# Accumulators in turn, earlier loads and pinned weight sums in the up projection of a decoder layer

## The chip, the core and the metric

The kernel runs on one core of a Trainium2 chip. The core has a matmul engine (PE, with its weight loads shown apart as PEld), a vector engine (DVE), an activation engine (ACT), a general engine (POOL, also called GpSimd) and a queue engine (SP) that issues transfers from device memory. Matmul results go to PSUM, here used as eight tiles of 128 x 512 float32 values (eight banks); PE writes them, and DVE and ACT read them. POOL reads and writes only the on-chip memory SBUF in this kernel. The metric is the device time of one execution in microseconds; lower is better. A comparison is by the median of several executions.

## What is computed

One decoder layer on 512 tokens of 1024 values: an RMS norm, two parallel token mixers (RWKV-7 and a sparse attention) with gates and an output projection, and then a gated MLP. The change lies in the first half of the MLP alone:

```python
h = rms_norm(x, norm_ffn_pre[l])
u = causal_dwconv(h @ ffn_up[l], ffn_conv_w[l], ffn_conv_b[l])
u_gate, u_val = jnp.split(u, 2, axis=-1)
x = x + rms_norm((jax.nn.silu(u_gate) * u_val) @ ffn_down[l], norm_ffn_post[l])
```

`ffn_up` is 1024 x 5632, which is 44 blocks of 128 output channels; the convolution is causal, three tokens wide, and runs on each channel by itself.

## The kernel before

**Precision.** A float32 product is made of three products in PE's faster format: each operand is split into a high part and the residue that the high part leaves, and high x high, high x low and low x high are added up in one accumulator. A split costs one copy on ACT (the high part) and one subtraction on POOL or DVE (the residue). `split_to` (L157) and `split_w` (L165) load a weight block from device memory in two halves through SP's queue and split them: copy on ACT (listed under L125), residue on POOL (L163). The raw halves, the high parts and the residues each have three buffers (WB = 3), so that about one and a half blocks of weights are held.

**The up stage.** The loop over `j` (L1592) takes 22 pairs of blocks; blocks 2j and 2j+1 are the gate and the value channels of one slice. For an ordinary block, `mm3` (L220 to L224) runs 24 matmuls of 512 columns into one accumulator `pu`, taken by `pj` from a ring of two. Blocks 0 to 2 are begun before the loop (`half_up`), in other accumulators. After each block come its convolution steps: an ACT pass with scale and bias (L1619) and two DVE passes that add the shifted tokens (L1620, L1621). All three read the accumulator, and the ring gives it to the next block but one only when they are done. After a pair come SiLU on ACT (L1625), the gated product on POOL (L1626), and the split of the product for the down projection on ACT and DVE (L1627, L1628).

**Half products.** For the pairs j = 7, 9, ..., 19 (`SEVEN`) the two blocks are not multiplied directly. `seven` (L1548) cuts the product of two weight blocks and the tokens into quarters and forms it with seven quarter-size products instead of eight (Winograd's scheme): 84 matmuls of 256 columns, into three accumulators named sg, sv and st from `px`, `py` and `pz`, rings of two each. Each of the seven products is a call of `prod` (L1559 to L1564). Three take plain weight quarters, split by `plain` (L1549 to L1554, into the buffers that ordinary blocks use); four take sums and differences of weight quarters, made by `seven_prep` (L1519 to L1546): four transfers of raw quarters `q` through SP's queue, four DVE passes (L1534, L1537, L1541, L1544), each followed by an ACT copy (L1530) and a DVE residue (L1531). Between products, DVE adds partial results (L1567); the add into `u2` reads the left half of st, whose right half is the target of the fourth product, and an accumulator is tracked as a whole. The token operands of the sums are the token forms (`token_forms`, L1483 to L1517), made once on DVE and ACT during blocks 4 to 11.

`seven_prep` is a generator that the loop advances: its loads and first sum are traced at the start of pair j - 1, the others after blocks of that pair.

**What sets the order.** The code is traced in program order, and a planner then writes a fixed order for each engine: going through time by its own cost estimates, an engine takes the ready instruction that was traced first. So an instruction whose inputs the planner believes to be there early is placed ahead of earlier traced ones that still wait. On the chip each engine runs its own list strictly in that order and waits where an input is late. `tc.keep_in_program_order(i)` binds instruction i to stand behind the one traced before it on its engine; instructions traced later may still be placed ahead of it. SBUF and PSUM buffers are given out in turn by tag, and the first write waits for the last reader of the buffer's previous content.

Of the kernel before, what the change touches and what calls it, by code (L numbers as in the profile page):

```python
# [10 lines left out]
F32 = mybir.dt.float32  # L11
F32R = mybir.dt.float32r
AF = mybir.ActivationFunctionType
OP = mybir.AluOpType
# [13 lines left out]
SEVEN = tuple(range(7, 20, 2))  # L28
# [15 lines left out]
def hybrid_layer(ctx: ExitStack, tc: tile.TileContext, a, out, dbg=None, stop=None):  # L44
    nc = tc.nc
    te, ve, sc, po, sy = nc.tensor, nc.vector, nc.scalar, nc.gpsimd, nc.sync

    def pool(name, side="left", c=None):
        p = tc.tile_pool(name=name, bufs=1, side=side, reuse_waits="tile")
        if c is None:  # L50
            return p
        return c.enter_context(p)
# [6 lines left out]
    def pj(name):  # L59
        return ps.tile([128, 512], F32, tag="pj", name=name, bufs=2)  # L60

    def px(name):
        return ps.tile([128, 512], F32, tag="px", name=name, bufs=2)

    def py(name):
        return ps.tile([128, 512], F32, tag="py", name=name, bufs=2)
# [11 lines left out]
    def pz(name):  # L78
        return pzs[-1][1].tile([128, 512], F32, tag="pz", name=name, bufs=2)
# [85 lines left out]
    def split_w(src, name, late=False):  # L165
        hs, ls = [], []
        for i in range(2):
            hi = wp.tile([128, 512], F32R, tag="whi", name=f"{name}h{i}", bufs=WB)
            lw = wp.tile([128, 512], F32R, tag="wlo", name=f"{name}l{i}", bufs=WB)
            split_to(src[:, i * 512:i * 512 + 512], hi, lw, f"{name}{i}", 512, late=late)  # L170
            hs.append(hi)
            ls.append(lw)
        return hs, ls
# [46 lines left out]
    def mm3(p, wh, wl, mh, ml, n=KT, first=True, last=True):  # L220
        for k in range(n):
            te.matmul(p, wh(k), mh(k), start=first and k == 0, stop=False)  # L222
            te.matmul(p, wh(k), ml(k), start=False, stop=False)  # L223
            te.matmul(p, wl(k), mh(k), start=False, stop=last and k == n - 1)  # L224
# [703 lines left out]
    for g in range(2):  # L928
        group_tiles(g)
        for i in range(GP):  # L930
            p = GP * g + i
# [326 lines left out]
    for p8 in range(8):  # L1258
        v = values(p8, os_[p8])
        s = score(p8 + 1, os_[p8 + 1]) if p8 < 7 else iter(())  # L1260
# [142 lines left out]
    op = pool("op", "left", octx)  # L1403
# [40 lines left out]
    def half_up(b, half):  # L1444
        wh, wl = (wslice(w) for w in up4[b])
        ts = slice(half * 256, half * 256 + 256)
        p = pu4[b][:, ts]
        for k in range(KT):
            te.matmul(p, wh(k), h2h[:, k, ts], start=k == 0, stop=False)
            te.matmul(p, wh(k), h2l[:, k, ts], start=False, stop=False)  # L1450
            te.matmul(p, wl(k), h2h[:, k, ts], start=False, stop=k == KT - 1)  # L1451
# [20 lines left out]
    with pool("ff") as ff:  # L1472
# [7 lines left out]
        def quarter(t, r, c):  # L1480
            return t[:, r * hf:(r + 1) * hf, (lft, rgt)[c]]
# [34 lines left out]
                    low(3, (1, 0))  # L1516
                    yield  # L1517

        def seven_prep(j, sw):  # L1519
            o = P()  # L1520
            o.raw = {}
            for r, c in ((1, 0), (1, 1), (0, 0), (0, 1)):
                q = o.raw[r, c] = sw.tile([128, 512], F32, tag=f"q{r}{c}", name=f"q{j}{r}{c}", bufs=1)
                sy.dma_start(q, a["up"][2 * j + r][:, c * 512:c * 512 + 512])
            s = sw.tile([128, 512], F32, tag="qs", name=f"qs{j}", bufs=1)
            o.w = {}

            def put(i, q):
                hi, lo = (sw.tile([128, 512], F32R, tag=f"s{i}{x}", name=f"s{j}{i}{x}", bufs=1) for x in "hl")
                sc.activation(hi, q, AF.Copy)  # L1530
                ve.tensor_tensor(lo, q, hi.bitcast(F32), op=OP.subtract)  # L1531
                o.w[i] = hi, lo

            ve.tensor_tensor(s, o.raw[1, 0], o.raw[1, 1], op=OP.add)  # L1534
            put(1, s)
            yield o
            ve.tensor_tensor(s, s, o.raw[0, 0], op=OP.subtract)  # L1537
            put(2, s)
            yield o
            q = o.raw[1, 0]  # L1540
            ve.tensor_tensor(q, o.raw[0, 0], q, op=OP.subtract)  # L1541
            put(3, q)
            yield o
            ve.tensor_tensor(s, o.raw[0, 1], s, op=OP.subtract)  # L1544
            put(4, s)
            yield o  # L1546

        def seven(j, o):  # L1548
            def plain(r, c, eng):  # L1549
                hi = wp.tile([128, 512], F32R, tag="whi", name=f"ph{j}{r}{c}", bufs=WB)  # L1550
                lo = wp.tile([128, 512], F32R, tag="wlo", name=f"pl{j}{r}{c}", bufs=WB)
                sc.activation(hi, o.raw[r, c], AF.Copy)  # L1552
                eng.tensor_tensor(lo, o.raw[r, c], hi.bitcast(F32), op=OP.subtract)  # L1553
                return hi, lo  # L1554

            def tok(r, c):
                return quarter(h2h, r, c), quarter(h2l, r, c)

            def prod(p, w, x, first=True, last=True):  # L1559
                for k in range(hf):  # L1560
                    ks = slice(k * 128, k * 128 + 128)
                    for n, (y, z) in enumerate(((0, 0), (0, 1), (1, 0))):
                        te.matmul(p, w[y][:, ks], x[z][:, k, :], start=first and k + n == 0,  # L1563
                                  stop=last and k == hf - 1 and n == 2, skip_group_check=True)  # L1564

            def add(o_, x, y):
                ve.tensor_tensor(o_, x, y, op=OP.add)  # L1567

            g, v, t = px(f"sg{j}"), py(f"sv{j}"), pz(f"st{j}")
            w11 = plain(0, 0, po)  # L1570
            prod(g[:, lft], w11, tok(0, 0))
            prod(t[:, lft], o.w[2], forms[1])
            u2, u4 = (sw.tile([128, 256], F32, tag=f"u{i}", name=f"su{i}{j}", bufs=1) for i in (2, 4))
            sc.activation(u2, g[:, lft], AF.Copy)
            add(u2, t[:, lft], u2)
            prod(v[:, rgt], o.w[1], forms[0])
            add(u4, v[:, rgt], u2)
            w12 = plain(0, 1, po)
            prod(t[:, rgt], o.w[3], forms[2])
            prod(g[:, lft], w12, tok(1, 0), first=False)  # L1580
            add(v[:, rgt], t[:, rgt], u4)
            prod(g[:, rgt], o.w[4], tok(1, 1))
            add(g[:, rgt], g[:, rgt], u4)
            w22 = plain(1, 1, ve)
            prod(t[:, rgt], w22, forms[3], first=False)
            add(v[:, lft], t[:, rgt], u2)
            return g, v

        side = tf = token_forms()
        sctx2 = ExitStack()  # L1590
        nxt = None
        for j in range(22):  # L1592
            us = []
            sv_ = None
            if j in SEVEN:
                for _ in side:
                    pass
                sv_ = seven(j, nxt)
            elif j + 1 in SEVEN:
                if j + 1 == SEVEN[0]:  # L1600
                    for _ in side:
                        pass
                    sw = pool("sw", "right", sctx2)
                side = seven_prep(j + 1, sw)
                nxt = next(side)
            for x in range(2):
                blk = 2 * j + x
                if blk < NU:
                    p = pu4[blk]
                    half_up(blk, 1)  # L1610
                elif sv_ is not None:
                    p = sv_[x]
                else:
                    wh, wl = after.get(blk) or split_w(a["up"][blk], f"up{blk}")
                    p = pj(f"pu{blk}")
                    mm3(p, wslice(wh), wslice(wl), lambda k: h2h[:, k, :], lambda k: h2l[:, k, :])
                cv = blk * 4
                u = ff.tile([128, S], F32, tag=f"u{x}", name=f"u{blk}", bufs=2)
                sc.activation(u, p, AF.Identity, scale=cvec[:, cv + 2:cv + 3], bias=cvec[:, cv + 3:cv + 4])  # L1619
                ve.scalar_tensor_tensor(u[:, 1:], p[:, :S - 1], cvec[:, cv + 1:cv + 2], u[:, 1:], op0=OP.mult, op1=OP.add)  # L1620
                ve.scalar_tensor_tensor(u[:, 2:], p[:, :S - 2], cvec[:, cv:cv + 1], u[:, 2:], op0=OP.mult, op1=OP.add)  # L1621
                us.append(u)
                if j > 1:
                    next(side, None)
            sc.activation(us[0], us[0], AF.Silu)  # L1625
            po.tensor_tensor(us[1], us[0], us[1], op=OP.mult)  # L1626
            sc.activation(ah[:, j, :], us[1], AF.Copy)  # L1627
            ve.tensor_tensor(al[:, j, :], us[1], ah[:, j, :].bitcast(F32), op=OP.subtract)  # L1628
            if j == 1:
                f4ctx.close()  # L1630
# [120 lines left out]
```

## Time and profile before

Three executions gave 1166.04, 1166.78 and 1168.3 us; the median is 1166.78.

| what | value |
|---|---|
| profiled execution, its own time | 1167.55 us |
| its span, first to last instruction | 1165.7 us |
| mean granted matmul clock over the span | 0.994 |
| PE busy | 1138.4 us |
| DVE busy | 657.4 us |
| ACT busy | 604.5 us |
| POOL busy | 539.6 us |

How to read the rows that follow in the prediction. A timeline row has the start, the duration, engine, line, operation, output <- input, shape and count; brackets give the engine's idle time just before and the event that ended it, as far as the profile can tell. A row of waits has who waited for whom: total, number of times, longest. A windows row has the stretch, its length, the busy time of PE, PEld, DVE, ACT and POOL, each with its number of instructions, the granted clock, the share of the transfer engines and GB/s. A group row has line, engine, operation, names, shapes and count, then the busy total in us, the mean of one in ns, and the idle time before them. Durations of matmuls overlap, so their pace is read from their starts. Releasers are inferred; where the engine named had long been done, it was another.

### The profile page before, as it was taken

The numbers are of one execution on the slowest core, as the hardware profiler recorded it, in microseconds if no ns is written. First come the engines' busy times: TensorE is split into PE (matmuls) and PEld (weight loads), VectorE is DVE, ScalarE is ACT, GpSimd is POOL, SyncE is SP. The second block draws the span as 40 slices with busy tenths as digits, with TensorE's granted clock in tenths as the row PEclk, the third lists the DMA queues.
The fourth block names the chain that finished last, engine by engine and source line by source line (L and its number), as shares of the span: only waits on it lengthen the run. The fifth ranks groups of instructions, "written<-read, shape, count | busy, mean of one in ns | idle before, by whom it ended". The sixth has DMA issues, their size and how long they took to land. (4 is left out here: it accounts for less than half of the span.)

```text
span 1165.7 us, 20396 instructions
## 1 busy us (share of the span) xinstructions
PE 1138.4 (98%) x7590; PEld 922.1 (79%) x7590; DVE 657.4 (56%) x1316; ACT 604.5 (52%) x1194; POOL 539.6 (46%) x516
## 2 busy tenths in 40 slices
PE   9999999999999999999999999999899999999997
PEld 7888887777888777667777778889678888888886
DVE  4246656735664833787887646556856766631103
ACT  6447664545665442676766644435444555543311
POOL 4346655335754533475454334302564345454430
PEclk9999999999999999899999999999999999999999
DMA  7422345322434752244622146611333233134421
GB/s 261 109 74 80 104 112 167 94 79 85 136 105 121 199 155 88 69 116 139 198 83 73 46 154 208 229 37 37 117 95 100 82 105 100 56 112 140 128 64 73
DMA packets 95509, 131.98 MB, mean 113 GB/s; under 512 B 34033, under 2 KB 36913, under 8 KB 95154
## 3 DMA queue, kind: packets, MB, share of 16 engines
q1 hardware_dynamic: 79554, 116.26, 33.0%
q10 hardware_dynamic: 15856, 14.42, 3.9%
q8 instruction: 60, 0.98, 0.4%
q14 instruction: 39, 0.32, 0.1%
HBM read 108.30 MB, written 19.14 MB: 109 GB/s over the span
## 5 line engine op out<-in xcount | busy, mean ns | idle before, releaser
L1121 ACT ACTIVATE p<-p,stt 128x384 f32<-128x384 f32 (+3 forms) x128 | 70.7, 554 | 35.4 <-DVE stt L1119 35.1
L1119 DVE CUSTOM_DVE_ANT_0 p<-s,rh 128x384 f32<-128x384 f32 (+3 forms) x128 | 59.2, 484 | 22.7 <-PE s L1105 18.9
L1093 POOL TENSOR_SCALAR p<-p,stt 128x512 f32<-128x512 f32 (+1 forms) x64 | 39.4, 627 | 40.5 <-DVE stt L1086 24.8
L141 PE MATMUL pt<-ident,p 128*128 128x128 f32 x320 | 44.7, 275 | 1.2 <-DVE p L1095 1.2
L141 PEld LDWEIGHTS pt<-ident,p 128*128 128x128 f32 x320 | 38.0, 141 | 6.8 <-DVE p L1095 1.6
L1112 PE MATMUL s<-kst,qs 128*128 128x512 f32 (+1 forms) x128 | 39.1, 397 | 2.4 <-DVE stt L1119 2.1
L1173 PE MATMUL o<-PT,vt 128*64 128x384 f32 (+3 forms) x256 | 41.0, 443 | 0.0
L1627 ACT ACTIVATE ah<-u 128x512 fp32r<-128x512 f32 x22 | 13.9, 632 | 46.5 <-POOL u L1626 46.5
L1620 DVE SCALAR_TENSOR_TENSOR u<-pu,cvec,u 128x511 f32<-128x511 f32 x30 | 22.4, 747 | 24.5 <-ACT u L1619 24.4
L1628 DVE TENSOR_TENSOR al<-u,ah 128x512 fp32r<-128x512 f32 x22 | 16.8, 765 | 33.4 <-ACT ah L1627 32.9
L1626 POOL TENSOR_TENSOR u<-u,u 128x512 f32<-128x512 f32 x22 | 29.8, 1353 | 10.6 <-DVE u L1621 9.6
L1095 DVE TENSOR_SCALAR p<-p,stt 128x512 f32<-128x512 f32 (+1 forms) x64 | 32.7, 537 | 0.7
L1164 ACT ACTIVATE PT<-pt 128x512 f32<-128x512 f32 x48 | 27.4, 587 | 10.4 <-PE pt L141 10.2
L1173 PEld LDWEIGHTS o<-PT,vt 128*64 128x64 f32 x256 | 16.3, 136 | 18.4 <-issue 16.1
L1112 PEld LDWEIGHTS s<-kst,qs 128*128 128x128 f32 x128 | 21.5, 191 | 11.1 <-DVE stt L1119 7.7
L1395 DVE TENSOR_TENSOR p2ss<-p2ss 128x1 f32<-128x1 f32 x4 | 0.6, 160 | 52.1 <-ACT p2jl L1393 52.1
L1166 DVE COPY PT<-pt 128x512 f32<-128x512 f32 x32 | 21.8, 681 | 8.6 <-PE pt L141 8.6
L1619 ACT ACTIVATE u<-pu,cvec 128x512 f32<-128x512 f32 x30 | 22.9, 763 | 3.0 <-PE pu L1451 3.0
L1121 ACT ACTIVATION_READ_ACCUMULATOR p<-p,stt 128x1 f32 x128 | 24.3, 190 | 0.0
L824 ACT ACTIVATE UV<-xs 64x256 f32<-64x256 f32 x16 | 6.0, 378 | 35.0 <-PE xs L819 34.6
L1621 DVE SCALAR_TENSOR_TENSOR u<-pu,cvec,u 128x510 f32<-128x510 f32 x30 | 22.4, 746 | 0.8
L1625 ACT ACTIVATE u<-u 128x512 f32<-128x512 f32 x22 | 13.9, 630 | 17.1 <-DVE u L1621 17.1
(1884 smaller groups left out, 4157.7 us busy)
## 6 DMA issues: line engine op xcount, KB each, us to landing
q<-in_up_dram SPq DMA_DIRECT2D x28, 256.0 KB, 2.9
gtd<-gt ACTq DMA_DIRECT2D x16, 256.0 KB, 2.2
qs<-qd SPq DMA_DIRECT2D x32, 128.0 KB, 3.4
g<-gtd SPq DMA_DIRECT2D x16, 256.0 KB, 3.0
xt<-in_x_dram SPq DMA_DIRECT2D x4, 512.0 KB, 5.8
bvd<-bv SPq DMA_DIRECT2D x8, 256.0 KB, 2.3
t<-oad SPq DMA_DIRECT2D x8, 256.0 KB, 2.9
x<-in_x_dram SPq DMA_DIRECT2D x4, 512.0 KB, 6.8
```

The source lines that it names most:

```text
L141: return te.transpose(o, i, ident)
L1093: po.tensor_scalar(o.pe[e, b, k], o.pe[e, b, k], w, 1.0, op0=OP.mult, op1=OP.mult)
L1095: ve.tensor_scalar(o.pe[e, b, k], o.pe[e, b, k], w, None, op0=OP.mult)
L1112: m = te.matmul(s_[:, :n], qt, kt[:, x, b, :n], start=x == 0, stop=x == 1)
L1119: ve.tensor_tensor_reduce(sb, parts[b], rh[e][:, (3 - qb) * 128:], -1.0, BIG, OP.add, OP.min, st[e][:, 0, i:i + 1])
L1121: sc.activation(sb, sb, AF.Exp, scale=-1.0, bias=st[e][:, 0, i:i + 1], accum_out=st[e][:, 1, i:i + 1])
L1164: sc.activation(m[e][:, :c], pt[:, :c], AF.Copy)
L1173: te.matmul(acc[e * 64:e * 64 + 64, j * 128:], vt[:, j, b * 256 + g * 64:b * 256 + g * 64 + 64], m[e][:, c:c + n], start=False, stop=k == ...
L1619: sc.activation(u, p, AF.Identity, scale=cvec[:, cv + 2:cv + 3], bias=cvec[:, cv + 3:cv + 4])
L1620: ve.scalar_tensor_tensor(u[:, 1:], p[:, :S - 1], cvec[:, cv + 1:cv + 2], u[:, 1:], op0=OP.mult, op1=OP.add)
L1621: ve.scalar_tensor_tensor(u[:, 2:], p[:, :S - 2], cvec[:, cv:cv + 1], u[:, 2:], op0=OP.mult, op1=OP.add)
L1626: po.tensor_tensor(us[1], us[0], us[1], op=OP.mult)
```

## The change

Four things are edited, in two functions and the loop.

- Ordinary up blocks with j < 7, that is blocks 3 to 13, take their accumulators from `pj`, `px`, `py` and `pz` in turn (two buffers each) and no longer from `pj` alone. From pair 7 on, ordinary blocks use `pj` as before.
- The loads of the raw quarters are a function of their own, `seven_load`. For the first group they are traced at the start of pair 6, as before; for a later group inside the group before it, behind the plain splits, not at the start of the pair between.
- The plain splits of a group are all traced at its start, and the third residue runs on POOL, not on DVE.
- The four sums are pinned with `keep_in_program_order`, and traced in two pairs. For the first group: sums 1 and 2 after block 12's convolution steps, sums 3 and 4 after block 13's. For later groups: sums 1 and 2 after the convolution steps of the group before, sums 3 and 4 after those of the block that follows it.

```diff
-        def seven_prep(j, sw):
+        def seven_load(j, sw):
             o = P()
-            o.raw = {}
-            for r, c in ((1, 0), (1, 1), (0, 0), (0, 1)):
+            o.raw, o.w = {}, {}
+            for r, c in ((1, 0), (0, 0), (0, 1), (1, 1)):
                 q = o.raw[r, c] = sw.tile([128, 512], F32, tag=f"q{r}{c}", name=f"q{j}{r}{c}", bufs=1)
                 sy.dma_start(q, a["up"][2 * j + r][:, c * 512:c * 512 + 512])
+            return o
+
+        def seven_prep(j, o, sw):
             s = sw.tile([128, 512], F32, tag="qs", name=f"qs{j}", bufs=1)
-            o.w = {}
-            def put(i, q):
+            def put(i, q, x, y, op):
+                tc.keep_in_program_order(ve.tensor_tensor(q, x, y, op=op))
                 hi, lo = (sw.tile([128, 512], F32R, tag=f"s{i}{x}", name=f"s{j}{i}{x}", bufs=1) for x in "hl")
                 sc.activation(hi, q, AF.Copy)
-                ve.tensor_tensor(lo, q, hi.bitcast(F32), op=OP.subtract)
                 o.w[i] = hi, lo
-            ve.tensor_tensor(s, o.raw[1, 0], o.raw[1, 1], op=OP.add)
-            put(1, s)
-            yield o
-            ve.tensor_tensor(s, s, o.raw[0, 0], op=OP.subtract)
-            put(2, s)
-            yield o
+                return ve.tensor_tensor(lo, q, hi.bitcast(F32), op=OP.subtract)
+            put(1, s, o.raw[1, 0], o.raw[1, 1], OP.add)
+            put(2, s, s, o.raw[0, 0], OP.subtract)
+            yield
             q = o.raw[1, 0]
-            ve.tensor_tensor(q, o.raw[0, 0], q, op=OP.subtract)
-            put(3, q)
-            yield o
-            ve.tensor_tensor(s, o.raw[0, 1], s, op=OP.subtract)
-            put(4, s)
-            yield o
+            put(3, q, o.raw[0, 0], q, OP.subtract)
+            put(4, s, o.raw[0, 1], s, OP.subtract)
+            yield
...
             g, v, t = px(f"sg{j}"), py(f"sv{j}"), pz(f"st{j}")
-            w11 = plain(0, 0, po)
+            w11, w12, w22 = (plain(r, c, po) for r, c in ((0, 0), (0, 1), (1, 1)))
+            nxt = seven_load(j + 2, sw) if j + 2 in SEVEN else None
             prod(g[:, lft], w11, tok(0, 0))
...
-            w12 = plain(0, 1, po)
...
-            w22 = plain(1, 1, ve)
...
-                sv_ = seven(j, nxt)
+                *sv_, nxt = seven(j, cur)
             elif j + 1 in SEVEN:
                 if j + 1 == SEVEN[0]:
                     for _ in side:
                         pass
                     sw = pool("sw", "right", sctx2)
-                side = seven_prep(j + 1, sw)
-                nxt = next(side)
+                    nxt = seven_load(j + 1, sw)
+                    cur, side = nxt, seven_prep(j + 1, nxt, sw)
...
-                    p = pj(f"pu{blk}")
+                    p = ((pj, px, py, pz)[blk % 4] if j < SEVEN[0] else pj)(f"pu{blk}")
...
+            if j in SEVEN and nxt:
+                cur, side = nxt, seven_prep(j + 2, nxt, sw)
+                next(side)
```

More of the change, by code (lines that the diff above doesn't have):

```diff
@@ L1583, in seven @@
             add(g[:, rgt], g[:, rgt], u4)
-            w22 = plain(1, 1, ve)
             prod(t[:, rgt], w22, forms[3], first=False)
             add(v[:, lft], t[:, rgt], u2)
-            return g, v
+            return g, v, nxt
         side = tf = token_forms()
```

## The prediction

> **What bounds the kernel now.** I read the page first, then the waits of the matmul engine in the up stage, then that engine's timeline row by row, and last the other engines' rows around each stall.
>
> ```profile
> PE 1138.4 (98%) x7590; PEld 922.1 (79%) x7590; DVE 657.4 (56%) x1316; ACT 604.5 (52%) x1194; POOL 539.6 (46%) x516
> ```
>
> PE is busy for 98% of the span, so only its stalls can be won, unless work leaves it; the change adds and removes no matmul. The edited code runs from about 796 to 1040 us. PE's waits there:
>
> ```profile
> PE pu L222 <- DVE u L1621: 5.6, 4, 2.9
> PE st L1563 <- DVE su L1567: 2.7, 6, 0.5
> PE sg L1563 <- POOL pl L1553: 2.1, 5, 0.4
> PE pu L222 <- ACT tf1h L1497: 1.7, 2, 1.0
> ```
>
> The first and fourth rows are up blocks ahead of the half products, the others lie inside the half products. Idle time understates a stall, because each matmul is drawn with its overlapping tail, so I measure stalls by starts. **Stage A**, blocks 5 to 13:
>
> ```profile
> 817.55 0.47 PE L222 MATMUL pu<-hh,up5h 128*128 128x512 f32 x1 [0.72 <-ACT tf1h L1497]
> 824.97 0.47 PE L222 MATMUL pu<-hh,up6h 128*128 128x512 f32 x1 [1.71 <-DVE u L1621]
> 831.68 0.47 PE L222 MATMUL pu<-hh,up7h 128*128 128x512 f32 x1 [0.98 <-ACT tf1h L1497]
> 837.82 0.47 PE L222 MATMUL pu<-hh,up8h 128*128 128x512 f32 x1 [0.46 <-DVE u L1621]
> 846.45 0.47 PE L222 MATMUL pu<-hh,up9h 128*128 128x512 f32 x1 [2.94 <-DVE u L1621]
> 850.39 0.63 PE L224 MATMUL pu<-hh,up9l 128*128 128x512 f32 x1
> 854.26 0.47 PE L222 MATMUL pu<-hh,up10h 128*128 128x512 f32 x1 [0.49 <-DVE u L1621]
> 870.66 0.39 PE L222 MATMUL pu<-hh,up13h 128*128 128x512 f32 x1
> 876.10 0.28 PE L1563 MATMUL sg<-hh,ph 128*128 128x256 f32 x1
> ...
> 816.68:876.10 59.42, 52.12 (x217) 41.40 (x217) 40.14 (x49) 28.31 (x47) 33.46 (x24) 0.97 0.33 105
> 876.10:885.85 9.75, 9.75 (x85) 9.75 (x84) 8.06 (x13) 5.09 (x9) 2.90 (x3) 1.00 0.27 82
> ```
>
> Block 13 takes 876.10 - 870.66 = 5.44 us, undisturbed. Nine such blocks are 48.96 us; the first windows row shows 59.42 from the end of block 4 to the first half product. Stage A loses 10.46 us. Its costliest stall is the 2.94 before block 9; after it the matmuls run slow for a while (0.63 instead of 0.39 each, up to the row at 850.39), and the window's granted clock is 0.97. The second windows row is the first group of half products, 84 matmuls in 9.75 us without a stall: 1.39 us for each of the seven products.
>
> **Stage B**, the other six groups of half products, one example (seven 11 and the blocks ahead of it):
>
> ```profile
> 907.60 0.40 PE L222 MATMUL pu<-hh,up20h 128*128 128x512 f32 x1
> 918.51 0.28 PE L1563 MATMUL sg<-hh,ph 128*128 128x256 f32 x1
> 919.33 0.38 PE L1563 MATMUL sg<-hh,pl 128*128 128x256 f32 x1 [0.43 <-POOL pl L1553]
> 923.96 0.39 PE L1563 MATMUL st<-tf2h,s113h 128*128 128x256 f32 x1 [0.45 <-DVE su L1567]
> 929.72 0.40 PE L222 MATMUL pu<-hh,up24h 128*128 128x512 f32 x1
> ```
>
> From 918.51 to 929.72 are 11.21 us against 9.75: 1.46 lost, about 0.72 at each bracket. The PE waits count five of the first kind and six of the second. So the first kind is worth 5 x 0.72 = 3.6 us and the second 6 x 0.73 = 4.4. All stalls that the change can reach: 10.46 + 8.0 = 18.5 us.
>
> **Accumulators in turn (blocks 3 to 13).** No instruction is added. Now block n waits until the convolution steps (L1620, L1621) have read block n-2; afterwards block n-8, so the six stalls lose their cause. What is late next are the weights, which pass through ACT (high part) and POOL (residue), in queues that also hold the gated product (L1626) and its copy (L1627), which wait for DVE's convolutions:
>
> ```profile
> 822.32 1.29 POOL L163 TENSOR_TENSOR up6l<-up60r,up6h 128x512 fp32r<-128x512 f32 x1 [2.54 <-issue]
> 829.03 1.30 POOL L163 TENSOR_TENSOR up7l<-up70r,up7h 128x512 fp32r<-128x512 f32 x1 [3.74 <-issue]
> 835.57 1.64 POOL L163 TENSOR_TENSOR up8l<-up80r,up8h 128x512 fp32r<-128x512 f32 x1 [1.87 <-PE pu L224]
> ...
> 842.95 0.69 DVE L1534 TENSOR_TENSOR qs<-q,q 128x512 f32<-128x512 f32 x1 [5.28 <-DMA q<-in_up_dram]
> ```
>
> The first residue of block 6 is ready at 823.61, of block 7 at 830.33, of block 8 at 837.21. With these kept, block 8 starts at 837.21 instead of 837.82: the early stalls give almost nothing, since DVE's backlog of token forms reaches PE through the weights. The row at 842.95 shows what made the largest stall: DVE stood 5.28 us at the first sum of weight quarters, waiting for a transfer, with block 7's convolution behind it. That sum moves behind block 12 (below) and the accumulators are there, so from block 8 on nothing holds PE: 837.21 + 6 x 5.44 = 869.85 for the first half product, against 876.10. Gain 6.2. Lower bound 3, if the weights after block 8 wait once more for about that long; upper bound 10.46, if the planner, which sees PE run earlier, also puts the weights earlier. I take 6.2, the value the rows give with the order kept.
>
> **Sums pinned.** The four sums of a group and their splits are the same eight DVE and four ACT instructions as before; only their place moves. A DVE pass costs 0.68, an ACT copy 0.62:
>
> ```profile
> L1537 DVE TENSOR_TENSOR qs<-qs,q 128x512 f32<-128x512 f32 x5 | 3.4, 680 | 0.0
> L1552 ACT ACTIVATE ph<-q 128x512 fp32r<-128x512 f32 x18 | 11.1, 617 | 0.0
> ...
> 872.03 0.75 DVE L1620 SCALAR_TENSOR_TENSOR u<-pu,cvec,u 128x511 f32<-128x511 f32 x1 [0.68 <-ACT u L1619]
> 877.47 0.75 DVE L1620 SCALAR_TENSOR_TENSOR u<-pu,cvec,u 128x511 f32<-128x511 f32 x1
> ```
>
> For group 7 they come late. The last row is block 13's convolution, 1.37 us after the first half product starts; in the new kernel sums 3 and 4 follow it. It ends about 2.9 after the start; sum 3, its copy and its residue take 0.68 + 0.62 + 0.68, so the residue is there at 4.9. The fourth product is due at 3 x 1.39 = 4.17 and wants the residue 0.25 later: 0.5 us of new wait, 1.0 with one of these passes held up by POOL. I take 1.0 (bounds 0 and 3, the latter if sum 2's residue, wanted at 1.6 and behind block 12's convolution at 872.03, is late too).
>
> From group 9 on, sums 1 and 2 follow the previous group's own convolutions, sums 3 and 4 the next block's. Now they stand ahead of those convolutions:
>
> ```profile
> L1619 ACT ACTIVATE u<-pu,cvec 128x512 f32<-128x512 f32 x30 | 22.9, 763 | 3.0 <-PE pu L1451 3.0
> ...
> 913.45 0.75 DVE L1621 SCALAR_TENSOR_TENSOR u<-sv,cvec,u 128x510 f32<-128x510 f32 x1
> 915.38 1.29 POOL L1626 TENSOR_TENSOR u<-u,u 128x512 f32<-128x512 f32 x1
> 916.71 0.63 ACT L1627 ACTIVATE ah<-u 128x512 fp32r<-128x512 f32 x1 [2.70 <-POOL u L1626]
> 917.99 2.54 POOL L1553 TENSOR_TENSOR pl<-q,ph 128x512 fp32r<-128x512 f32 x2 [1.32 <-issue]
> ...
> 923.50 0.41 DVE L1567 TENSOR_TENSOR su<-st,su 128x256 f32<-128x256 f32 x1
> ```
>
> The group ended on PE at 907.60, its last convolution on DVE at 914.20. POOL's product, ACT's copy and the first plain weight's residue follow, at 919.28, where PE waits. With the sums behind, the convolution is done about 3.1 us after PE (an add 0.41, ACT 0.76, two passes of 0.75, and 0.4 between, an estimate from the gaps of these rows), so this whole chain comes 3.5 us earlier and the first kind of wait goes: 3.6 us gained. Lower bound 0, if the planner keeps the plain copy behind the same work.
>
> The second kind: the add of 923.50 must release the bank before the fourth product. Count from 907.60: convolutions to 3.1, sums 1 and 2 with copies 3.96 to 7.1, block 20's convolution to 8.6, sums 3 and 4 to 12.6, block 21's to 14.1, the add to 14.5. Due at 10.88 + 4.17 = 15.05. Slack half a microsecond, less than one held-up pass. I take half of the present wait: 2.2 us gained, bounds +4.4 and a loss (the slower rival).
>
> **Third plain residue on POOL, loads mid-group.** Seven residues move from DVE (0.69) to POOL (1.29):
>
> ```profile
> L1553 POOL TENSOR_TENSOR pl<-q,ph 128x512 fp32r<-128x512 f32 x12 | 15.2, 1291 | 7.9 <-issue 7.9
> L1553 DVE TENSOR_TENSOR pl<-q,ph 128x512 fp32r<-128x512 f32 x6 | 4.2, 692 | 7.7 <-ACT ph L1552 7.7
> 907.95:930.07 22.12, 21.24 (x134) 18.95 (x133) 15.62 (x25) 11.67 (x21) 10.21 (x9) 1.00 0.32 96
> ```
>
> POOL goes from 10.2 to 11.5 of 22 us, and that weight serves the last product only, so it costs nothing by itself; with no cover it would be 7 x 1.29 = 9. The four loads of a group pass SP's queue during the previous group, where the fourth can stand until the third residue is done; up weights are issued behind it. I price that at nothing, bounds 0 and one 1.29 per group. The gain is the transfer that DVE no longer waits for, already counted.
>
> Against this move speaks a pair of rows:
>
> ```profile
> 929.72 1.29 POOL L163 TENSOR_TENSOR up24l<-up241r,up24h 128x512 fp32r<-128x512 f32 x1 [4.58 <-ACT up24h L125]
> 929.82 1.73 DVE L1544 TENSOR_TENSOR qs<-q,qs 128x512 f32<-128x512 f32 x1
> ```
>
> A DVE pass of 0.68 that starts while POOL works ends only after it: 1.05 more. [...]
>
> **Sum.** 6.2 - 1.0 + 3.6 + 2.2 = 11.0 us. The profiled execution took 1167.55 (span 1165.7 and 1.85 around it), giving 1156.55; it lay 0.77 above the median of the runs, 1166.78, from which the sum gives 1155.8. I say **1156.0**.
>
> **Rivals.** (1) Everything goes: 18.5 less 1.0 is 17.5, so 1149. For it: PE's work is untouched; against: the weight rows above. (2) The wait only changes its name: weights in stage A leave 3 of the gain, the second wait of stage B stays whole, group 7 loses 1.0: 3 - 1.0 + 3.6 = 5.6, less a further 1.5 if the second wait grows by a quarter microsecond a group: 1162.7. For it: the DVE backlog in the weight rows. (3) Slower: sums 3 and 4 delay the bank's release. Place: DVE between the convolution of the block after a group and the add at L1567. If all four passes there are held up by POOL (4 x 1.05 = 4.2 against a slack of 0.5), PE waits 3.7 instead of 0.73 in each of six groups: 17.8 lost, against 6.2 + 3.6 - 1.0 = 8.8 kept, so 9.0 slower: 1175.8. With n held-up passes a group waits 1.05 n - 0.5; at two that is 1.6, worse than now, and it eats all gains from 2.2 us a group, between two and three passes. For it: the half microsecond; against: DVE is busy 15.62 us in 22.12, and a pass can be fitted in while ACT copies. (4) It does not do what it says: the planner hoists other work before the pins and the stalls return elsewhere: 1166.8.
>
> **How the numbers follow.** The forecast 0.48, rival 1 0.17, rival 2 0.20, rival 3 0.08, rival 4 0.07. About 0.2%, 2.3 us, is what a measurement of this kernel tells from no change. So faster 0.85, same 0.07, slower 0.08. The range from 1148.5 to 1163 leaves out rivals 3 and 4 and the tails.
>
> **What would show it.** Right: no wait of PE for L1621 in up5 to up10, only waits for residues (L163) up to block 8; the first half product near 870; its group longer than 9.75 by about 1; later groups without the wait for L1553 and with a smaller one for L1567. Wrong: stalls of 2 us or more left before block 9, later groups longer than 11.2, or a wait for the quarters' sums (s3) in every group.

## The result and the profile after

The changed kernel takes **1178.37 us** (median of five executions, 1174.61 to 1181.03); the kernel before took 1167.13 beside it (1166.04 to 1168.3). The ratio is 1.0095, with a 95% interval from 1.0069 to 1.0121: about 11 us slower, where 11 us faster was forecast. The profiled execution took 1178.37 (span 1176.6), against 1167.55 (span 1165.7).

Lines of the edited part have shifted: in the changed kernel the products are L1560 (L1563 before), the adds L1564 (L1567), the convolution steps L1615 to L1617 (L1619 to L1621), the gated product and its split L1625 to L1627, the sums L1531, their copies L1533 and residues L1535, the plain copies and residues L1549 and L1550.

The page's line of busy time, and the three longest of PE's waits from 796 to 1050 us, of the changed kernel:

```profile
PE 1141.1 (97%) x7590; PEld 923.6 (78%) x7590; DVE 656.8 (56%) x1309; ACT 606.4 (52%) x1194; POOL 560.3 (48%) x523
```

```profile
PE st L1560 <- DVE su L1564: 16.4, 6, 3.0
PE pu L224 <- POOL up8l L163: 1.0, 1, 1.0
PE st L1560 <- ACT s73h L1533: 1.0, 1, 1.0
```

All four waits that the prediction started from have changed. The two ahead of the half products and the one for `pl` are gone. The one for the add into `su` has grown from 2.7 to 16.4, as often as before.

Where the time lies is read from the first matmul of block 3 (ahead of it, executions differ by up to 4 us in a stretch that the edits do not touch). PE's timeline, chosen rows of the kernel before and then of the changed one; `dn` is the first matmul of the down projection:

```profile
805.78 0.40 PE L222 MATMUL pu<-hh,up3h 128*128 128x512 f32 x1
...
1039.89 0.39 PE L1347 MATMUL dn<-dnw00h,ah 128*128 128x512 f32 x1
```

```profile
806.46 0.40 PE L222 MATMUL pu<-hh,up3h 128*128 128x512 f32 x1
870.27 0.28 PE L1560 MATMUL sg<-hh,ph 128*128 128x256 f32 x1
909.16 0.40 PE L222 MATMUL pu<-hh,up20h 128*128 128x512 f32 x1
920.07 0.28 PE L1560 MATMUL sg<-hh,ph 128*128 128x256 f32 x1
924.11 0.28 PE L1560 MATMUL sv<-tf0h,s111l 128*128 128x256 f32 x1
927.05 0.39 PE L1560 MATMUL st<-tf2h,s113h 128*128 128x256 f32 x1 [2.67 <-DVE su L1564]
932.80 0.40 PE L222 MATMUL pu<-hh,up24h 128*128 128x512 f32 x1
1050.45 0.39 PE L1347 MATMUL dn<-dnw00h,ah 128*128 128x512 f32 x1
```

Stage A, from block 3 to the first half product, takes 870.27 - 806.46 = 63.8 us, where the kernel before took 876.10 - 805.78 = 70.3: **6.5 gained**. From there to the down projection are 180.2 us, against 163.8: **16.4 lost**. The stall before the fourth product of group 11 is the row at 927.05. Stretches of the changed kernel (group 7 with block 16, and the groups 9, 11 and 19):

```profile
870.27:888.68 18.41, 16.28 (x110) 14.56 (x108) 13.30 (x19) 8.30 (x14) 8.50 (x7) 1.00 0.33 101
894.12:909.16 15.04, 11.67 (x86) 11.27 (x84) 9.44 (x14) 6.84 (x12) 7.19 (x5) 0.89 0.28 88
920.07:932.80 12.73, 10.06 (x86) 9.87 (x84) 7.38 (x12) 5.91 (x10) 6.54 (x5) 1.00 0.34 104
1014.63:1028.66 14.03, 11.36 (x86) 11.16 (x84) 7.47 (x12) 5.91 (x10) 6.53 (x5) 0.88 0.07 20
```

Group 7 and block 16 took 9.75 + 5.44 = 15.2 before, so 3.2 are lost there. Groups 11 to 17 take 12.73 each instead of 11.21. Group 19 takes 1.3 more again, at a granted clock of 0.88; group 9 takes 2.3 more, at 0.89 and with 0.7 more of waiting.

Why the add is late is seen on DVE, in the changed kernel from the last convolution of group 9 to the add for group 11, and then three of POOL's passes beside them:

```profile
911.92 0.75 DVE L1617 SCALAR_TENSOR_TENSOR u<-sv,cvec,u 128x510 f32<-128x510 f32 x1
912.59 0.68 DVE L1531 TENSOR_TENSOR qs<-q,q 128x512 f32<-128x512 f32 x1
913.97 1.00 DVE L1535 TENSOR_TENSOR s111l<-qs,s111h 128x512 fp32r<-128x512 f32 x1 [0.70 <-ACT s111h L1533]
916.82 0.69 DVE L1627 TENSOR_TENSOR al<-u,ah 128x512 fp32r<-128x512 f32 x1 [1.85 <-ACT ah L1626]
917.42 0.69 DVE L1531 TENSOR_TENSOR qs<-qs,q 128x512 f32<-128x512 f32 x1
918.03 0.74 DVE L1616 SCALAR_TENSOR_TENSOR u<-pu,cvec,u 128x511 f32<-128x511 f32 x1
918.81 1.01 DVE L1535 TENSOR_TENSOR s112l<-qs,s112h 128x512 fp32r<-128x512 f32 x1
919.74 0.74 DVE L1617 SCALAR_TENSOR_TENSOR u<-pu,cvec,u 128x510 f32<-128x510 f32 x1
920.40 1.12 DVE L1531 TENSOR_TENSOR q<-q,q 128x512 f32<-128x512 f32 x1
922.22 0.69 DVE L1535 TENSOR_TENSOR s113l<-q,s113h 128x512 fp32r<-128x512 f32 x1 [0.70 <-ACT s113h L1533]
922.83 0.68 DVE L1531 TENSOR_TENSOR qs<-q,qs 128x512 f32<-128x512 f32 x1
924.21 1.01 DVE L1535 TENSOR_TENSOR s114l<-qs,s114h 128x512 fp32r<-128x512 f32 x1 [0.70 <-ACT s114h L1533]
925.14 0.74 DVE L1616 SCALAR_TENSOR_TENSOR u<-pu,cvec,u 128x511 f32<-128x511 f32 x1
925.91 0.75 DVE L1617 SCALAR_TENSOR_TENSOR u<-pu,cvec,u 128x510 f32<-128x510 f32 x1
926.58 0.41 DVE L1564 TENSOR_TENSOR su<-st,su 128x256 f32<-128x256 f32 x1
```

```profile
912.64 1.78 POOL L163 TENSOR_TENSOR up21l<-up211r,up21h 128x512 fp32r<-128x512 f32 x1 [1.29 <-ACT up21h L125]
914.38 1.73 POOL L1625 TENSOR_TENSOR u<-u,u 128x512 f32<-128x512 f32 x1
922.84 1.83 POOL L1550 TENSOR_TENSOR pl<-q,ph 128x512 fp32r<-128x512 f32 x1 [1.87 <-ACT ph L1549]
```

Counted from the group's end at 909.16, the add ends at 17.8; the prediction had 14.5, against a due time of 15.05. Three things make the difference: DVE stands 1.85 and then runs `al` (0.60 to the next start) before sum 2; four passes of the sums take 1.00 to 1.12 instead of 0.68; and each residue but the second waits 0.70 for its ACT copy with nothing in between (these copies were in the count). POOL's passes are stretched as well, to 1.7 and 1.8 instead of 1.29. Residue of block 21, gated product, `ah` and `al` follow one another, so the stretch of the first two (0.49 and 0.44) makes `al` 0.9 later: half of the 1.85. The other half is the chain itself.

### The profile page after: what moved, and what is told of

It is laid out like the page before. It is cut to its first block, busy times and chain, and to the rows that moved or that the text cites. A ratio compares the mean times of both kernels' runs of the same rounds, so it can differ in the third digit from the quotient of the medians.

```text
span 1176.6 us, 20388 instructions
## 1 busy us (share of the span) xinstructions
PE 1141.1 (97%) x7590; PEld 923.6 (78%) x7590; DVE 656.8 (56%) x1309; ACT 606.4 (52%) x1194; POOL 560.3 (48%) x523
## 5 line engine op out<-in xcount | busy, mean ns | idle before, releaser
L1550 POOL TENSOR_TENSOR pl<-q,ph 128x512 fp32r<-128x512 f32 x21 | 34.6, 1649 | 24.6 <-ACT ph L1549 24.6
L1625 POOL TENSOR_TENSOR u<-u,u 128x512 f32<-128x512 f32 x22 | 32.4, 1472 | 11.6 <-DVE u L1617 10.7
L1627 DVE TENSOR_TENSOR al<-u,ah 128x512 fp32r<-128x512 f32 x22 | 17.2, 784 | 34.6 <-ACT ah L1626 34.6
L1164 ACT ACTIVATE PT<-pt 128x512 f32<-128x512 f32 x48 | 27.4, 586 | 10.4 <-PE pt L141 10.2
L1615 ACT ACTIVATE u<-pu,cvec 128x512 f32<-128x512 f32 x30 | 22.9, 762 | 3.0 <-PE pu L1451 3.0
L1617 DVE SCALAR_TENSOR_TENSOR u<-pu,cvec,u 128x510 f32<-128x510 f32 x30 | 22.3, 745 | 0.6
```

## The experiments

**Theory P**: the pins cost the time, because they put the sums' passes ahead of convolutions and of the add into `su`. **Rivals**: the bank alone is at fault (`st` held by the add); the hole before `al` (theory Q); passes of DVE and POOL that hold each other up; the accumulators or the loads.

**1. Accumulators alone**, on the kernel before:

```diff
-                    p = pj(f"pu{blk}")
+                    p = ((pj, px, py, pz)[blk % 4] if j < SEVEN[0] else pj)(f"pu{blk}")
```

> The kernel before with one part of the change alone: blocks 3 to 13 take their accumulators from the four rings in turn. Theory A (the gain of the accumulators is their own, the stalls of the half products are not touched): the first half product comes at about 870 instead of 876.1, the later groups stay at 11.2 us each with both small waits, so about 1161. Rival (the accumulators gain only because the sums no longer stand in DVE's queue at 843, 5.28 us long, ahead of block 7's convolution): block 9 or a block after it waits again for weights behind that stand, first half product at 873 or later, 1164 to 1167.

Measured: 1163.53 us, ratio 0.9969 (0.9958 to 0.9981). Stage A takes 68.6 instead of 70.3. The wait for DVE's convolution is gone, but PE now waits for weights: 0.7 and 0.7 before the low parts of blocks 6 and 7, 1.0 at block 8, 1.1 and 0.6 at block 9. The early sum, which DVE stands at for its transfer, still delays the weights through ACT. So the accumulators by themselves are worth 1.7 of the 6.5, and the rival has the mechanism: block 9 waits for weights. (The medians differ by 3.5. The profiled executions show 1.75 from block 3 on, and the groups are unchanged; the rest is not explained.)

**2. The change without them**, the rest as changed:

```diff
-                    p = ((pj, px, py, pz)[blk % 4] if j < SEVEN[0] else pj)(f"pu{blk}")
+                    p = pj(f"pu{blk}")
```

> The changed kernel with all ordinary blocks on pj again: what the accumulators in turn are worth in it. If they and the moved sums each take a part of stage A: the stall before block 9 is gone (the sums stand behind block 12) but the waits before blocks 5 to 8 are back, 4 to 5 us more than the changed kernel, 1182. If the moved sums alone bring the gain of stage A: no change, 1178.

Measured: 1178.42 us, ratio 1.0099 (1.0077 to 1.0122). Stage A takes 64.8, one us more than with the turn of accumulators. The stall before block 9 is gone here too. The time does not move: the accumulators' 1.0 is too little to show in it. By the profiled executions, 5.5 of the 6.5 come from moving the first group's sums out of block 8's way, and the accumulators add 1.0.

**3. The change without the pins**:

```diff
-                tc.keep_in_program_order(ve.tensor_tensor(q, x, y, op=op))
+                ve.tensor_tensor(q, x, y, op=op)
```

> The changed kernel without the pins; the sums are traced where the change puts them. Theory P (the pinned place of the sums ahead of the next block's convolution delays DVE's add into u2 and with it the fourth product): the wait for L1564 falls from 2.7 us to half a microsecond or less in every group, the groups take 11 us or less instead of 12.7 to 15, about 1160. [...]

Measured: **1156.61 us**, ratio 0.9907 (0.9889 to 0.9925): this one edit turns a kernel that was 11 us slower into one that is 10 us faster. In the waits of this run no row for `su` or `pl` is left. DVE, from the middle of group 9 to the add of group 11 (block 20 starts at 903.02, the first half product of group 11 at 913.92):

```profile
899.79 0.69 DVE L1535 TENSOR_TENSOR s111l<-qs,s111h 128x512 fp32r<-128x512 f32 x1
...
901.32 0.69 DVE L1531 TENSOR_TENSOR qs<-qs,q 128x512 f32<-128x512 f32 x1
...
906.17 0.68 DVE L1535 TENSOR_TENSOR s114l<-qs,s114h 128x512 fp32r<-128x512 f32 x1
...
908.21 0.75 DVE L1617 SCALAR_TENSOR_TENSOR u<-sv,cvec,u 128x510 f32<-128x510 f32 x1
...
917.34 0.42 DVE L1564 TENSOR_TENSOR su<-st,su 128x256 f32<-128x256 f32 x1
```

Left to itself, the planner runs three of the four sums during the half products of the group before (group 9 starts at 893.01), where DVE has little else. The convolutions then end 5.9 after the group's end (in the changed kernel 3.5), and yet the add starts at 14.3, in time. Groups 11 to 19 take 9.8 to 10.3. Group 7's sums go back to block 8, and stage A takes 67.1.

**4. Which part took the two small waits away?** No pins, and the third plain residue back on DVE:

```diff
-            w11, w12, w22 = (plain(r, c, po) for r, c in ((0, 0), (0, 1), (1, 1)))
+            w11, w12 = (plain(r, c, po) for r, c in ((0, 0), (0, 1)))
+            w22 = plain(1, 1, ve)
```

> The changed kernel without pins and with the third plain residue on DVE as before. Theory P: the move of that residue is a small matter, groups of 10 to 10.5 us, 1156 to 1159. Rival (taking the residue from DVE is what removes the small wait for the add into u2): the wait of 0.45 us comes back in every group, 10.8 us, 1161.

Measured: 1161.0 us, ratio 0.9956 (0.9942 to 0.997). Both waits are back, and the stretch from the first half product to the down projection takes 163.8 us, as in the kernel before; without this edit (run 3) it takes 157.2. DVE of this run:

```profile
913.76 0.69 DVE L1550 TENSOR_TENSOR pl<-q,ph 128x512 fp32r<-128x512 f32 x1 [1.28 <-ACT ph L1549]
914.42 0.75 DVE L1617 SCALAR_TENSOR_TENSOR u<-pu,cvec,u 128x511 f32<-128x511 f32 x1
```

The residue stands 1.28 for its ACT copy, ahead of the convolution that precedes the add. Moving it to POOL is worth 6.6 us in these stretches, without pins; the earlier loads and the new place of the plain splits are worth nothing there. (The medians differ by 4.4: stage A happened to be 1.1 shorter in run 4.)

**5. The bank.** The changed kernel, with products 4 and 7 in an accumulator of their own from `pj`:

```diff
-            prod(t[:, rgt], o.w[3], forms[2])
+            t2 = pj(f"su2{j}")
+            prod(t2[:, rgt], o.w[3], forms[2])
...
-            prod(t[:, rgt], w22, forms[3], first=False)
+            prod(t2[:, rgt], w22, forms[3], first=False)
```

> The changed kernel, with the fourth and the seventh product in an accumulator of their own from the ring pj, so that the fourth product need not wait for the add that reads the other half of st. Theory P with the bank as its last link: the wait before the fourth product goes, and DVE is late for nothing else by more than 1 us (the seventh product starts 4 us later): groups of 9.8 to 10.5 us, about 1159, and the runs lie closer together because PE no longer stands near 3 us. Rival D (DVE as a whole is too late in these groups): the stall moves to the seventh product or to the next group, 1170 or more.

Measured: 1165.15 us, ratio 0.9991 (0.9981 to 1.0001). The wait changes its place:

```profile
PE su L1560 <- DVE sv L1564: 7.1, 6, 1.8
```

The fourth product runs, and the seventh waits, 1.05 in most groups, for a later add behind the same passes of DVE. Groups 11 to 19 take 11.1 instead of 12.7 to 14.0, and the time lies between the two theories: the bank makes the wait earlier and longer, but with a bank of its own PE still meets a lateness that is DVE's.

**6. Sum 4 later**: a `yield` between `put(3, ...)` and `put(4, ...)`, so that sum 4 is pinned behind the second convolution after a group.

```diff
             put(3, q, o.raw[0, 0], q, OP.subtract)
+            yield
             put(4, s, o.raw[0, 1], s, OP.subtract)
```

> The changed kernel with sum 4 and its split moved from behind the first block's convolution to behind the second block's; sum 3 stays. Theory P: one sum, its residue and DVE's wait for the copy between them leave the queue ahead of the add (0.69 + 0.70 + 1.0), sum 4 itself may stay ahead of it (0.69): the wait falls from 2.7 to about 1 us, 1178 - 6 x 1.7 = about 1168. [...]

Measured: 1176.99 us, ratio 1.0085 (1.007 to 1.01); the wait for `su` is 11.7 in total, 1.9 in most groups, where about 1 was expected. The planner still runs sum 4 itself ahead of the add (1.05, stretched), so only its residue and the wait for its copy left the stretch, and DVE then stands 0.50 for ACT ahead of block 21's convolution: the add comes forward by 0.7. That the time falls by 1.4 only has a second reason: four of the six groups ran at a granted clock of 0.87 to 0.88 and took 13.5 to 14.5, the other two 12.0 at 1.00 (mean over the span 0.991, in the changed kernel 0.995).

**7. `al` later**: in the pairs of half products, `al` pinned behind sum 2's residue.

```diff
-            ve.tensor_tensor(al[:, j, :], us[1], ah[:, j, :].bitcast(F32), op=OP.subtract)
+            i = ve.tensor_tensor(al[:, j, :], us[1], ah[:, j, :].bitcast(F32), op=OP.subtract)
+            if j in SEVEN and nxt:
+                tc.keep_in_program_order(i)
```

> The changed kernel with one order more: the residue of the gated product (al, L1627) of a pair of half products is pinned behind the second sum's residue. Theory Q (sum 2 comes late because the list has it behind al, which waits 1.85 us for POOL's product and ACT's copy): that hole is filled with sum 2, the add into u2 comes 1.5 to 2 us earlier, PE's wait for it falls from 2.7 to about 1 us, about 1167. [...]

Measured: 1176.54 us, ratio 1.008 (1.006 to 1.01); the wait stays at 2.65 (3.53 in group 9). DVE and then ACT, this run:

```profile
915.85 0.75 DVE L1616 SCALAR_TENSOR_TENSOR u<-pu,cvec,u 128x511 f32<-128x511 f32 x1 [1.34 <-ACT u L1615]
...
917.11 1.78 DVE L1627 TENSOR_TENSOR al<-u,ah 128x512 fp32r<-128x512 f32 x1
```

```profile
913.99 0.63 ACT L1626 ACTIVATE ah<-u 128x512 fp32r<-128x512 f32 x1 [2.22 <-POOL u L1625]
...
915.05 0.76 ACT L1615 ACTIVATE u<-pu,cvec 128x512 f32<-128x512 f32 x1
```

The hole opens again one step later: ACT's convolution pass of block 20 stands behind `ah` in ACT's list, and `ah` waits for POOL. And `al` itself now collides with POOL (1.78 instead of 0.69). Theory Q falls: DVE's place for `al` is not what makes the add late. The chain from POOL to `ah` is late here too.

**8. Holes for the copies closed**: both sums of a pair first, then both residues, with a buffer of its own for sum 2 (no residue then waits for a copy just begun).

```diff
-                return ve.tensor_tensor(lo, q, hi.bitcast(F32), op=OP.subtract)
+                return lambda: ve.tensor_tensor(lo, q, hi.bitcast(F32), op=OP.subtract)
...
-            put(1, s, o.raw[1, 0], o.raw[1, 1], OP.add)
-            put(2, s, s, o.raw[0, 0], OP.subtract)
+            s2 = sw.tile([128, 512], F32, tag="qt", name=f"qt{j}", bufs=1)
+            low = [put(1, s, o.raw[1, 0], o.raw[1, 1], OP.add), put(2, s2, s, o.raw[0, 0], OP.subtract)]
+            for f in low:
+                f()
...
-            put(3, q, o.raw[0, 0], q, OP.subtract)
-            put(4, s, o.raw[0, 1], s, OP.subtract)
+            low = [put(3, q, o.raw[0, 0], q, OP.subtract), put(4, s2, o.raw[0, 1], s2, OP.subtract)]
+            for f in low:
+                f()
```

> The changed kernel, its sums pinned as they are, but the second sum gets a buffer of its own, and of each pair both sums come first on the vector engine and then both residues, so that no residue waits for its activation-engine copy: the passes are the same, the holes are gone. In the changed kernel three holes of 0.70 (ahead of the residues of sums 1, 3 and 4) lie between the end of a group and the add into u2. Theory H (idle holes on the vector engine make most of the lateness): the add comes up to 2.1 us earlier, the wait of 2.67 at the fourth product falls to 0.6 to 1.2, groups 11 to 17 take 10.4 to 10.9 instead of 12.7, and the time is 1165 to 1168. Theory L (the load itself and the other engines' queues set it; a hole that is closed reopens ahead of a convolution pass, as when the residue of the gated product was pinned late): the wait stays at 2.2 or more and the time at 1174 to 1178.

Measured: 1165.52 us, ratio 0.9995 (0.9982 to 1.0007). The wait falls from 2.67 to 1.60 in each of six groups, and behind it their matmuls start 0.12 apart, 11.7 each. (Those of group 7 do not: it waits 2.09 for sum 3's copy, its matmuls then start 0.21 apart for 3.7, and it takes 13.7.) DVE of this run:

```profile
906.44 1.67 DVE L1531 TENSOR_TENSOR qt<-qs,q 128x512 f32<-128x512 f32 x1
908.03 1.77 DVE L1535 TENSOR_TENSOR s111l<-qs,s111h 128x512 fp32r<-128x512 f32 x1
...
913.53 1.79 DVE L1531 TENSOR_TENSOR qt<-q,qt 128x512 f32<-128x512 f32 x1
```

The time lies in theory H's range, but by luck: the wait lies between the two theories (1.2 and 2.2), and the groups take 11.7 against theory H's 10.4 to 10.9. 2.1 of holes closed gave 1.07; another 3.6 of the gain came in groups 9 and 19, most of it by the clock (0.89 and 0.88 there in the changed kernel). Three passes now take about 1.7 instead of 0.68: the passes that were moved into the holes meet POOL.

**9. Fewer collisions**: the residues of the second and third plain quarters left out (the high part stands in their place, so that the output lacks these terms).

```diff
+                sc.activation(hi, o.raw[r, c], AF.Copy)
+                if c:
+                    return hi, hi
...
-                sc.activation(hi, o.raw[r, c], AF.Copy)
```

> The changed kernel without the residues of the second and third plain weight quarters (two of the three passes of the general engine at L1550 in each group; the matmuls read the high part in their place, so the output lacks these terms). The three rows that these residues touch on the vector engine in the changed kernel are 1.01, 1.12 and 1.01 long instead of 0.68. Theory S (collisions with the general engine stretch the chain of sums): the add into u2 comes 0.9 to 1.2 us earlier, the wait of 2.67 falls to 1.5 to 1.8, groups 11 to 17 take about 11.7, and the time is 1171 to 1173. Theory L: the vector engine waits for the activation engine instead, the wait stays at 2.4 or more, and the time is 1176 to 1179.

Measured: 1172.53 us, ratio 1.0049 (1.0033 to 1.0065). The wait falls to 1.98 (1.22 in group 9), between the two theories, so two POOL passes less are worth 0.7 of DVE's lateness in a group. Two of the three stretched rows are back, from 1.12 to 0.68 and from 1.01 to 0.69, which is the 0.7; the residue of sum 2 stays at 1.01. That the time lies in theory S's range is luck: in four of the six groups, of 13.6 each, the matmuls behind the wait start 0.21 apart for some time (granted clock 0.88 in group 11, below); the other two take 12.1.

**10. Pins for group 7 alone**, its four sums at the start of pair 6:

```diff
-                tc.keep_in_program_order(ve.tensor_tensor(q, x, y, op=op))
+                ins = ve.tensor_tensor(q, x, y, op=op)
+                if j == SEVEN[0]:
+                    tc.keep_in_program_order(ins)
...
+                    for _ in side:
+                        pass
```

> The changed kernel with pins for the first group alone, whose four sums are traced at the start of pair 6, behind block 11; the later groups' sums are not pinned. Theory P: stage A keeps the whole gain of the change (63.8 us from block 3 to the first half product against 70.3 before), group 7 runs in 9.8 us without the three waits for its sums, the later groups as in the run without pins (10.0 to 10.1): about 3 us under that run, 1153 to 1154. Rival (the sums at any place beside blocks 12 and 13 cost PE): group 7 still loses 2 to 3 us, 1156.

Measured: 1156.58 us, ratio 0.9917 (0.9891 to 0.9943). Stage A keeps its 63.8; group 7 takes 14.8, with 3.2 of waiting for `su` and a granted clock of 0.88: the sums start only behind `al` of the pair before, and so stand ahead of block 13's convolution and of the add. It is the same mechanism in another place. On DVE in this run, 3.9 and 2.1 us are idle ahead of it, around block 11's convolution.

**11. Group 7's sums into that idle time**: quarters loaded at the start of pair 5, sums pinned behind the convolutions of blocks 10 and 11, later groups not pinned (the condition in `put` is that of run 10).

```diff
-            elif j + 1 in SEVEN:
-                if j + 1 == SEVEN[0]:
-                    for _ in side:
-                        pass
-                    sw = pool("sw", "right", sctx2)
-                    nxt = seven_load(j + 1, sw)
-                    cur, side = nxt, seven_prep(j + 1, nxt, sw)
+            elif j + 2 == SEVEN[0]:
+                for _ in side:
+                    pass
+                sw = pool("sw", "right", sctx2)
+                nxt = seven_load(j + 2, sw)
+                cur, side = nxt, seven_prep(j + 2, nxt, sw)
```

> No pins from group 9 on; for group 7 the quarters are loaded one pair earlier, and its sums pinned behind the convolutions of blocks 10 (sums 1, 2) and 11 (sums 3, 4), where the vector engine stood idle for 3.9 and 2.1 us in the kernel that pinned the sums of group 7 alone. Theory P (a pinned sum costs only where its passes are ahead of a convolution or an add that the matmul engine waits for): the first half product stays at 63.8 after block 3's start, group 7 takes 9.75 to 10.3 instead of 14.8, the others 10.0, and the time is 1151 to 1153. Rival: the earlier loads hold up the weights of blocks 11 and 12 in the queue or the vector engine waits for a transfer again; then stage A loses 2 us or more and the time is 1155 or more.

Measured: **1153.14 us**, ratio 0.9888 (0.9865 to 0.9911), faster than both kernels. All of PE's waits from 796 to 1050, and then the first group:

```profile
PE pu L224 <- POOL up8l L163: 1.0, 1, 1.0
PE pu L224 <- POOL up6l L163: 0.7, 1, 0.7
PE pu L224 <- POOL up7l L163: 0.7, 1, 0.7
```

```profile
866.58:876.33 9.75, 9.75 (x85) 9.75 (x84) 6.39 (x12) 5.41 (x10) 4.56 (x5) 1.00 0.31 100
```

Stage A takes 63.8, group 7 its bare 9.75, the later groups about 10. Pins are not bad as such: the same four sums, pinned two blocks earlier, cost nothing.

## Why the prediction was wrong

**Accumulators and stage A: right.** 6.2 were forecast, 6.5 came, and the weights of blocks 6 to 8 wait as the prediction's rows said. It booked the 6.2 under the accumulators, but its rows gave the stalls up to block 8 only 0.6 (837.82 - 837.21) and named the sum that DVE stood at for the rest. The runs agree: the accumulators give 1.0 beside the rest and 1.7 alone (runs 2 and 1), the moved sum 5.5.

**Group 7's late sums: under-sized.** Priced at 1.0 with a bound of 3; 3.2 were lost. Three products wait (0.66 for sum 2's residue, 0.99 for sum 3's copy, 0.48 for sum 4's residue), not one.

**The first kind of wait: gone, as forecast (3.6), but the pins were not needed for it.** The step said that it goes because the sums leave the place ahead of the convolutions. Run 3 has the sums there and no such wait; run 4 has it back with the third plain residue on DVE. Whether the pins alone would also remove it, with that residue on DVE, no run shows. Of moving the third plain residue to POOL the prediction said "it costs nothing by itself" and saw only its cost. The row of the kernel before with 7.7 us of DVE idle at L1553 for six passes, quoted there, held the gain: 1.28 of standing and 0.69 of work a group, ahead of a convolution and of the add.

**The step that failed: the count to the add.** The prediction had the add done at 14.5, due at 15.05, with a slack of half a microsecond; it was done at 17.8. From the rows: the group's convolutions make way 0.3 later than counted (912.59 - 909.16 = 3.4 against 3.1); `al` and its wait cost 2.45; four stretched passes cost 1.4; against that, sum 2's copy is covered by a convolution pass (-0.6), and the passes overlap a little (-0.25). The sum is 3.3, which is the measured lateness. The count had DVE's sums and convolutions, but left out the other pass of the same stretch (`al`), and that its source runs through POOL and ACT, whose passes get later when the sums collide with POOL. So rival 3 is what happened, in its place: the add for the bank, on DVE behind the next block's convolution. Its mechanism is a part of it only: the four held-up passes cost 1.4 and not 4.2, the wait and pass of `al` 2.45. PE waits 2.67 to 3.02 against the 3.7 that it gave. That the total, 1178.4, comes near its 1175.8 is partly luck, since group 7 and the clock made up for the smaller wait. Its chance of 0.08 was far too low: the slack was under one pass, and the prediction itself quoted a pass of 1.73.

No single item of that count is the cause: pinning `al` later gained nothing, closing the copies' holes 1.07 of 2.1, two POOL passes less 0.7. The runs show a common cause, though: take the sums out of this stretch, as run 3 does, and the wait is zero. The add then starts at 14.3 and not much earlier, since it follows block 21's convolution, which follows PE. The stretch had no room for four sums, and the half products, in which DVE has idle time, did.

**Sum.** Forecast 6.2 - 1.0 + 3.6 + 2.2; measured from block 3 on: 6.5 - 3.2 - 13.2 = -9.9. The 13.2, which already hold the gain of the first kind, are 1.5 in each of six groups, 9.2 together, and 4.0 more in groups 9 and 19, most of it the lower clock. The prediction had noted slow matmuls behind a stall (0.63 instead of 0.39, block 9), but its sum put them at nothing. The profiled executions differ by 10.8, of which 0.7 lie ahead of block 3 and 0.3 behind the up stage.

## What to carry over

Before a pin moves work from one place to another, list every pass of that engine in the new stretch up to the next thing that PE waits for, with the waits on other engines in it; if the slack is less than one pass, expect a loss. An order that a planner found may look wrong where a transfer holds it up, and be right elsewhere: cure the one place (load earlier, pin there) and leave the other groups alone. And a pass that stands waiting on the engine which releases PE can be worth moving even to a slower engine (here 1.29 instead of 0.69).

## What was not expected of the hardware

**Short stalls slow the matmuls that follow, but not always.** In the changed kernel, after the stall of 3.02 in group 9 the 256-column matmuls start 0.21 apart instead of 0.12 for about 3 us, and the granted clock from 902.08 to 905.30 is 0.54; after 2.67 in group 19 the same (0.56 from 1021.61 to 1024.90); after 2.67 in groups 11 to 17 they do not (1.00 from 927.05 to 930.30, group 11). In run 9, 1.99 of idle was enough, in one group of run 5 even 1.81 (mean clock of that execution 0.995, up to 0.999 in others of the run); after the 1.60 of run 8 it did not happen in six groups. PE of run 9 in group 11, and the stretch of that group:

```profile
919.61 0.38 PE L1562 MATMUL st<-tf2h,s113h 128*128 128x256 f32 x1 [1.99 <-DVE su L1566]
919.83 0.28 PE L1562 MATMUL st<-tf2l,s113h 128*128 128x256 f32 x1
...
920.86 0.41 PE L1562 MATMUL st<-tf2h,s113h 128*128 128x256 f32 x1
```

```profile
913.06:926.91 13.85, 11.86 (x86) 11.61 (x85) 6.96 (x13) 5.81 (x10) 3.81 (x3) 0.88 0.29 96
```

Here the slow matmuls begin a microsecond after PE has resumed, and the granted clock of the whole stretch is 0.88. What decides it no run shows: of the five stalls of 2.67 in the changed kernel one had slow matmuls behind it and four had none. The slow matmuls make such a stall cost 1.3 us (group 19) to 2.8 us (a group of 15.54 in run 2, against 12.73) more than its idle time, and it may be why the executions of the changed kernel spread over 6 us (argued, not tested).

**Collisions of DVE and POOL stretch both.** From group 9 on, those of DVE's sums and residues that start during a pass of POOL take 1.0 to 1.8 instead of 0.68, POOL's passes up to 1.83 instead of 1.29; with two of POOL's passes left out (run 9), two of the stretched rows are back at 0.68 and 0.69. The convolution steps, which read PSUM and SBUF, stay at 0.75 beside the same POOL passes (0.74 at 918.03, beside POOL's 1.83 from 917.43). So a pass that is moved into idle time of DVE can be longer there than where it came from (run 8: 1.67 to 1.79).
